# Two transformer blocks: the normalization between projections on one PSUM tile, five tiles ahead of it, and the gated product on VectorE

## The chip, the cores and the metric

One core of a Trainium2 chip runs the whole program. The metric is the device time of one execution in microseconds (us), lower is better.

## The reference

Input x is 256 tokens of 1024 features, float32. A first block (attention, a gated linear recurrence and a differential attention, merged by gates) and two layers of a second block follow each other. All of them end in the same way: an output projection is added to x, x is normalized, and a gated feed-forward part with a short causal convolution follows. For the second block:

```python
    mix = jnp.einsum('bsd,de->bse', merged, w_o)
    x = layer_norm(ALPHA * x + mix, ln1_g, ln1_b)
    up = causal_dwconv_2(jnp.einsum('bsd,df->bsf', x, w_up), ffn_conv_w)
    a, b = jnp.split(up, 2, axis=-1)
    ffn = jnp.einsum('bsf,fd->bsd', jax.nn.silu(a) * b, w_down)
    return layer_norm(ALPHA * x + ffn, ln2_g, ln2_b)
```

The first block has RMS norms (no mean), GELU in place of SiLU and a bias in the convolution. The feed-forward width is 2816, 22 tiles of 128, for the gate and as many for the value.

## The kernel before, in words

x lies in SBUF with the features on the partitions: 8 tiles (`x[:, k]`) of 128 features x 256 tokens. All weights come as one stream of 128 x 128 tiles in the order of use. A piece of 8 tiles (512 KB) is loaded from SP's queue into one of six raw buffers and split into a rounded part `whi` (ScalarE, L186) and a rest `wlo` (VectorE, L187), with five buffers each. `W.begin(t0, n)` splits what tiles t0 to t0+n need and up to two pieces more (L193). One product of 8 weight tiles with 8 activation tiles is 24 matmuls, since `mm3` (L342) multiplies hi by hi, hi by lo and lo by hi. Activations are split in the same way (`split`, L353): `hh` (ScalarE) and `hl` (VectorE) for x.

A scheduler orders the instructions of each engine: it takes the source's order as priority and its own estimates of readiness, so an instruction that is ready can pass one that comes earlier in the source. PSUM has eight tiles of 128 x 512 (`ps`); a tile is free when its last reader is done.

**The seam** (`seam`, L476) joins an output projection (`prev`), a norm and the first tiles of the next projection (`nxt`). For each of the 8 output tiles it adds the product to x (L886 or L889), splits x times the norm's gain into zh and zl (L509, L510) and adds x and its square to running sums (`Norm.add`, L390: squares on ScalarE, sums on GpSimd for m < 7, on VectorE for m = 7). The next projection does not wait for the norm: its first NAHEAD = 4 tiles are multiplied with zh and zl, which lack only the factor 1/std (and the mean's share), one value per token. After the first of these tiles TensorE adds the sums over the partitions (`stats`, L417 and L418). Then follows a chain of small steps of 128 x 256 (L423 to L432, L467 to L474): the square of the mean on ScalarE, the mean, the variance, 1/sqrt from ScalarE with one Newton step on VectorE. `apply` (L447) makes the normalized x, hh and hl from it, tile by tile. The first two centring subtractions run on VectorE, the others on GpSimd; the product with rstd on VectorE (L454, L457 or L439); gain and bias on ScalarE. Only then do the tiles that ran ahead leave PSUM, times rstd (L532); with a LayerNorm GpSimd adds the mean's term (L538). The rest of `nxt` is multiplied with hh and hl, up to two tiles side by side.

There are seven seams: one at the start without a projection ahead of it, five between, and one at the end, whose norm (`finish`, L434) writes the result out. Three have a projection of 8 tiles ahead of them (w_out, twice w_o), three the down projection of 22.

**The up projection** (`ffn_up`, L910) computes gate tile j and value tile j by turns. Evacuation of a tile: a scaled copy on ScalarE (L919, L921), two shifted multiply-adds on VectorE (L922, L923), for a gate the activation function on ScalarE (L926). Gate times value runs on GpSimd (L929), for the last pair on VectorE (L932). The split of the product into fh and fl (L355, L356) is put off to the next tile's evacuation (`late`, `settle`). The down projection reads fh and fl of all 22 tiles in order.

## Time and profile before

| | us |
|---|---|
| median of 3 runs | 1213.05 |
| lowest and highest run | 1207.31, 1213.48 |
| the profiled execution | 1208.3 |
| its span | 1206.3 |

The profile shows the one execution of 1208.3 us; its times count from the start of its span. PE is TensorE, PEld its weight loads, DVE is VectorE, ACT ScalarE, POOL GpSimd, SP the engine whose queue issues the loads. A start and a duration in a timeline are in us; neighbours on one engine overlap a little, since the next instruction begins while the last one drains. PEclk is the granted TensorE clock of a stretch, 1.00 being 2.4 GHz.

### The profile page before, as it was taken

The numbers are of one execution on the slowest core, as the hardware profiler recorded it, in microseconds if no ns is written. First come the engines' busy times: TensorE is split into PE (matmuls) and PEld (weight loads), VectorE is DVE, ScalarE is ACT, GpSimd is POOL, SyncE is SP. The second block draws the span as 40 slices with busy tenths as digits, with TensorE's granted clock in tenths as the row PEclk, the third lists the DMA queues.
The fourth block names the chain that finished last, engine by engine and source line by source line (L and its number), as shares of the span: only waits on it lengthen the run. The fifth ranks groups of instructions, "written<-read, shape, count | busy, mean of one in ns | idle before, by whom it ended". The sixth has DMA issues, their size and how long they took to land.

```text
span 1206.3 us, 25236 instructions
## 1 busy us (share of the span) xinstructions
PE 1165.5 (97%) x9928; PEld 1146.3 (95%) x9928; DVE 956.2 (79%) x1767; ACT 763.7 (63%) x1391; POOL 245.0 (20%) x233
## 2 busy tenths in 40 slices
PE   8999999999999999999999999999999998999895
PEld 8999899999999999999998999999999998999895
DVE  7989886797988856886789988757995888977754
ACT  7678566756767645676557766556776565855542
POOL 2022020001122200120023222222420042222122
PEclk9999999999999999999999999999999998999898
DMA  7654445475466665545554566664455554565541
GB/s 284 224 168 155 166 143 168 127 229 189 148 212 202 196 207 192 162 154 175 184 184 142 165 210 203 209 193 148 151 189 177 185 166 135 155 203 185 189 141 35
DMA packets 60486, 212.61 MB, mean 176 GB/s; under 512 B 6864, under 2 KB 9296, under 8 KB 60368
## 3 DMA queue, kind: packets, MB, share of 16 engines
q1 hardware_dynamic: 60080, 210.88, 54.3%
q8 instruction: 77, 1.26, 0.4%
q10 hardware_dynamic: 288, 0.14, 0.1%
q14 instruction: 41, 0.34, 0.1%
HBM read 209.94 MB, written 1.05 MB: 175 GB/s over the span
## 4 chain that ended last, share of the span: by engine, by line
PE 65%; DVE 17%; ACT 9%; issue 5%; POOL 3%; DMA 0%; SPq 0%; POOLq 0%; ACTq 0%; DVEq 0%
PE ps L344 20%; PE ps L343 20%; PE ps L345 20%; DVE wlo L187 7%; ACT whi L186 4%; POOL wrk L929 2%; DVE R L510 1%; DVE wrk L923 1%; DVE wrk L922 1%; ACT a_lg L580 1%; PE ps L563 1%; PE ps L760 1%; PE ps L761 1%; PE ps L759 1%; DVE wrk L454 1%
## 5 line engine op out<-in xcount | busy, mean ns | idle before, releaser
L187 DVE TENSOR_TENSOR wlo<-raw,whi 128x1024 fp32r<-128x1024 f32 (+1 forms) x401 | 496.3, 1240 | 118.5 <-ACT whi L186 113.1
L343 PE MATMUL ps<-hh,whi 128*128 128x256 f32 x1912 | 536.5, 281 | 5.1 <-ACT hh L461 3.6
L344 PE MATMUL ps<-hl,whi 128*128 128x256 f32 x1912 | 532.0, 279 | 3.2 <-DVE hl L462 3.1
L186 ACT CAST whi<-raw 128x1024 fp32r<-128x1024 f32 (+1 forms) x401 | 414.6, 1038 | 186.8 <-PE ps L344 135.5
L345 PE MATMUL ps<-hh,wlo 128*128 128x256 f32 x1912 | 531.3, 278 | 0.6 <-DVE wlo L187 0.4
L343 PEld LDWEIGHTS ps<-hh,whi 128*128 128x128 f32 x1912 | 361.6, 189 | 8.3 <-ACT hh L461 4.0
L344 PEld LDWEIGHTS ps<-hl,whi 128*128 128x128 f32 x1912 | 362.1, 190 | 4.4 <-DVE hl L462 4.0
L345 PEld LDWEIGHTS ps<-hh,wlo 128*128 128x128 f32 x1912 | 361.1, 189 | 1.0 <-DVE wlo L187 1.0
L343 PE MATMUL ps<-R,whi 128*128 128x256 f32 (+1 forms) x1180 | 330.2, 281 | 6.8 <-ACT R L355 3.8
L344 PE MATMUL ps<-R,whi 128*128 128x256 f32 (+1 forms) x1180 | 329.5, 280 | 5.2 <-DVE R L510 3.5
L345 PE MATMUL ps<-R,wlo 128*128 128x256 f32 (+1 forms) x1180 | 327.9, 279 | 0.4 <-DVE wlo L187 0.2
L343 PEld LDWEIGHTS ps<-R,whi 128*128 128x128 f32 x1180 | 223.6, 190 | 9.0 <-ACT R L355 4.5
L344 PEld LDWEIGHTS ps<-R,whi 128*128 128x128 f32 x1180 | 223.5, 189 | 7.5 <-DVE R L510 4.9
L345 PEld LDWEIGHTS ps<-R,wlo 128*128 128x128 f32 x1180 | 223.1, 189 | 1.3 <-DVE wlo L187 1.2
L929 POOL TENSOR_TENSOR wrk<-wrk 128x256 f32<-128x256 f32 x63 | 82.9, 1316 | 238.6 <-DVE wrk L923 150.3
L355 ACT CAST R<-wrk 128x256 fp32r<-128x256 f32 x89 | 36.0, 407 | 117.5 <-POOL wrk L929 95.3
L405 POOL TENSOR_TENSOR n_sq<-n_sq,n_q 128x256 f32<-128x256 f32 x42 | 39.5, 941 | 169.1 <-ACT n_q L396 167.9
L922 DVE SCALAR_TENSOR_TENSOR wrk<-ps,par,wrk 128x255 f32<-128x255 f32 x120 | 56.6, 476 | 17.3 <-ACT wrk L921 17.3
L356 DVE TENSOR_TENSOR R<-wrk,R 128x256 fp32r<-128x256 f32 x89 | 38.9, 440 | 27.0 <-ACT R L355 26.9
L923 DVE SCALAR_TENSOR_TENSOR wrk<-ps,par,wrk 128x254 f32<-128x254 f32 x120 | 57.1, 477 | 1.6
L611 POOL TENSOR_SCALAR a_lg<-a_lg,a_r 128x256 f32<-128x256 f32 x24 | 25.3, 1056 | 113.1 <-DVE a_r L586 60.9
L509 ACT ACTIVATE R<-x,par 128x256 fp32r<-128x256 f32 x48 | 23.8, 507 | 27.8 <-DVE x L889 16.0
(225 smaller groups left out, 1088.7 us busy)
## 6 DMA issues: line engine op xcount, KB each, us to landing
raw<-in_wst SPq DMA_DIRECT2D x395, 512.0 KB, 4.0
x<-in_xT SPq DMA_DIRECT2D x4, 256.0 KB, 4.8
out_y<-x SPq DMA_DIRECT2D x3, 256.0 KB, 2.2
cst<-in_cst SPq DMA_DIRECT2D x1, 406.0 KB, 8.9
raw<-in_wst SPq DMA_DIRECT2D x1, 384.0 KB, 5.5
par<-in_par SPq DMA_DIRECT2D x1, 312.5 KB, 8.5
raw<-in_wst SPq DMA_DIRECT2D x1, 256.0 KB, 2.7
out_y<-x SPq DMA_DIRECT2D x2, 128.0 KB, 2.0
```

The source lines that it names most:

```text
L186: self.nc.scalar.copy(hi[:, a:b], w[:, a:b])
L187: self.nc.vector.tensor_sub(lo[:, a:b], w[:, a:b], hi[:, a:b].bitcast(F32))
L343: T.matmul(out, sh, mh, start=first, stop=False, skip_group_check=skip)
L344: T.matmul(out, sh, ml, start=False, stop=False, skip_group_check=skip)
L345: T.matmul(out, sl, mh, start=False, stop=last, skip_group_check=skip)
L355: A.copy(hi, src)
L356: V.tensor_sub(lo, src, hi.bitcast(F32))
L405: e.tensor_add(self.sq, self.sq, q)
L611: (G if i else V).tensor_scalar(pe[:, c], pe[:, c], r[:, i:i + 1], None, op0=OP.mult)
L922: V.scalar_tensor_tensor(y[:, 1:], p[:, :S - 1], pr(cw, 44 + i), y[:, 1:], op0=OP.mult, op1=OP.add)
L923: V.scalar_tensor_tensor(y[:, 2:], p[:, :S - 2], pr(cw, i), y[:, 2:], op0=OP.mult, op1=OP.add)
L929: G.tensor_tensor(y, held.pop(j), y, op=OP.mult)
```

## The change

`stats` keeps the whole chain in the PSUM tile of the sums: the variance, the squared root and 1/std are written there, and each of these steps on VectorE reads at most one tensor from SBUF; the square of the root moves to ScalarE, and an activation of one column with the next phase's function (`func`) follows it. A copy of 1/std goes to SBUF (`rs`) for the tiles that ran ahead. Centring reads the sum from PSUM for the first two tiles; gain and bias of every second tile move to VectorE. In the seams after a projection of 8 tiles the running sums are added on VectorE. Five tiles run ahead instead of four; three of them leave PSUM after the fourth, sixth and eighth step of the normalization and two behind it, and the mean's term is added on VectorE through the PSUM tile of the sums. Two tiles follow side by side in the up projections (7 tiles belong to a seam instead of 5) and in `win` (7 instead of 6). The weight pieces are split at other places: one call ahead of the statistics, none more with the later tiles, and one piece each after the third and the sixth step (`more`). In the up projection every product of gate and value runs on VectorE.

```diff
-NWIN = 6
+NWIN = 7
...
-NAHEAD = 4
+NAHEAD = 5
...
+    def more(self):
+        if self.splits < min(self.npc, self.low + NPC):
+            self.split()
...
-        def add(self, m, last=False):
+        def add(self, m, last=False, e=None):
...
-            e = G if m < 7 else V
+            e = e or (G if m < 7 else V)
...
-            v = wrk()
+            self.rstd, self.s1p = q[:, :S], p[:, S:]
+            f, v, y = self.rstd, wrk(), wrk()
             if self.ln:
                 self.mu, m2 = tmp("n_mu", [P, S], 1), wrk()
...
+                A.activation(m2, self.s1p, AF.Square, scale=1.0 / D)
+                V.tensor_scalar(self.mu, self.s1p, 1.0 / D, None, op0=OP.mult)
+                V.scalar_tensor_tensor(f, f, 1.0 / D, m2, op0=OP.mult, op1=OP.subtract)
+                V.tensor_scalar(v, f, 0.0, LN_EPS, op0=OP.max, op1=OP.add)
             else:
-                V.tensor_scalar(v, p[:, :S], 1.0 / D, RMS_EPS, op0=OP.mult, op1=OP.add)
-            self.rstd, self.done = rsqrt(v, tmp("n_r", [P, S], 1))
-            if self.ln and not last:
-                self.nmr = tmp("n_nm", [P, S], 1)
-                V.scalar_tensor_tensor(self.nmr, self.mu, -1.0, self.rstd, op0=OP.mult, op1=OP.mult)
+                V.tensor_scalar(v, f, 1.0 / D, RMS_EPS, op0=OP.mult, op1=OP.add)
+            A.activation(y, v, AF.Abs_reciprocal_sqrt)
+            A.activation(f, y, AF.Square)
+            if self.func is not None:
+                A.activation(tbl, f[:, :1], self.func)
+            V.scalar_tensor_tensor(f, f, -0.5, v, op0=OP.mult, op1=OP.mult)
+            self.done = V.scalar_tensor_tensor(f, f, 1.5, y, op0=OP.add, op1=OP.mult)
+            if not last:
+                self.rs = tmp("n_r", [P, S], 1)
+                A.copy(self.rs, self.rstd)
+
+        def center(self, k, d):
+            if k < 2:
+                V.scalar_tensor_tensor(d, self.s1p, -1.0 / D, x[:, k], op0=OP.mult, op1=OP.add)
+            else:
+                G.tensor_sub(d, x[:, k], self.mu)
+
+        def affine(self, k, e):
+            g, b = self.g[:, k:k + 1], self.b[:, k:k + 1]
+            if k % 2:
+                V.tensor_scalar(x[:, k], e, g, b, op0=OP.mult, op1=OP.add)
+            else:
+                A.activation(x[:, k], e, AF.Identity, scale=g, bias=b)
...
-        def apply(self):
-            for k in range(NT):
...
+        def apply(self, k):
...
+                d = wrk()
+                self.center(k, d)
+                V.tensor_tensor(e, d, self.rstd, op=OP.mult)
+                self.affine(k, e)
...
             if prev:
-                norm.add(m, not nxt)
+                norm.add(m, not nxt, V if prev[0][1] == 8 else None)
...
+        at = 0 if prev else 2
         for i, mt in enumerate(ahead):
-            W.begin(mt["t0"], 8)
+            if i > at + 1:
+                W.begin(mt["t0"], 8, None, 0)
+            elif i <= at:
+                W.begin(mt["t0"], 8)
...
-            if i == (0 if prev else 2):
+            if i == at:
                 for m in range(0 if prev else NT):
                     norm.add(m)
+                W.begin(ahead[i + 1]["t0"], 8, mt["t0"])
                 norm.stats()
-                norm.apply()
-        for mt, p in zip(ahead, out):
+        ts, gbs = [], tmp("n_gb", [P, 16], 1)
+
+        def leave():
+
+            mt, p = ahead[len(ts)], out[len(ts)]
             t = mt["into"] if "into" in mt else wrk()
-            V.tensor_tensor(t, p[:, :S], norm.rstd, op=OP.mult)
+            V.tensor_tensor(t, p[:, :S], norm.rs, op=OP.mult)
+            gb = None
             if norm.ln:
-                gb = tmp("n_gb", [P, 2], 2)
+                gb = gbs[:, 2 * len(ts):2 * len(ts) + 2]
                 A.copy(gb, p[:, S:width])
-                u = wrk()
-                A.activation(u, norm.nmr, AF.Identity, scale=gb[:, 0:1], bias=gb[:, 1:2])
-                G.tensor_add(t, t, u)
+            ts.append((t, gb))
+        for k in range(NT):
+            norm.apply(k)
+            if k in (2, 5):
+                W.more()
+            if k in (3, 5, 7):
+                leave()
+        while len(ts) < len(ahead):
+            leave()
+        if norm.ln:
+            nmr = tmp("n_nm", [P, S], 1)
+            V.scalar_tensor_tensor(nmr, norm.mu, -1.0, norm.rs, op0=OP.mult, op1=OP.mult)
+        for mt, (t, gb) in zip(ahead, ts):
+            if norm.ln:
+                u = norm.s1p
+                A.activation(u, nmr, AF.Identity, scale=gb[:, 0:1], bias=gb[:, 1:2])
+                V.tensor_tensor(t, t, u, op=OP.add)
             if "evac" in mt:
                 mt["evac"](t)
...
-                elif j < FT - 1:
-                    G.tensor_tensor(y, held.pop(j), y, op=OP.mult)
-                    late.append(lambda: split(fh[j], fl[j], y))
                 else:
                     V.tensor_tensor(y, held.pop(j), y, op=OP.mult)
-                    split(fh[j], fl[j], y)
+                    late.append(lambda: split(fh[j], fl[j], y))
+                    if j == FT - 1:
+                        settle()
...
-    n1 = Norm(False, pr("norm_ffn_g", 0, 8), to_x=False)
+    n1 = Norm(False, pr("norm_ffn_g", 0, 8), to_x=False, func=AF.Gelu_apprx_tanh)
...
-    seam(outs("w_out", 0, 8, mg), add_x, n1, up[:5], (8, 6))
+    seam(outs("w_out", 0, 8, mg), add_x, n1, up[:7], (8, 6))
...
-    phase(up[5:])
+    phase(up[7:])
```

The two norms before an up projection in the second block ask for SiLU in the same way (and take `up[:7]`), the two before `win` ask for Exp; `finish` uses `center` and `affine` too.

## Rows read from the trace of the kernel before

**Rows 1.** The page: busy time, share of the span and instructions of each engine.
```profile
PE 1165.5 (97%) x9928; PEld 1146.3 (95%) x9928; DVE 956.2 (79%) x1767; ACT 763.7 (63%) x1391; POOL 245.0 (20%) x233
```

**Rows 2.** Windows: length, busy us (count) of PE, PEld, DVE, ACT, POOL; PEclk, DMA share, GB/s.
```profile
276.00:297.00 21.00, 19.49 (x166) 18.83 (x164) 18.41 (x25) 15.76 (x27) 5.08 (x6) 1.00 0.56 178
622.00:643.00 21.00, 19.83 (x163) 18.98 (x162) 19.57 (x28) 15.73 (x28) 14.25 (x12) 0.98 0.54 170
643.00:660.00 17.00, 15.49 (x116) 15.01 (x115) 15.28 (x30) 11.47 (x24) 5.00 (x7) 0.92 0.33 116
828.50:845.50 17.00, 15.28 (x112) 14.85 (x111) 16.25 (x33) 11.67 (x27) 6.89 (x8) 0.90 0.35 118
976.00:1001.50 25.50, 22.65 (x178) 22.01 (x177) 20.77 (x26) 15.37 (x26) 13.41 (x12) 0.93 0.54 170
1001.50:1019.00 17.50, 14.01 (x97) 13.51 (x95) 15.35 (x29) 10.98 (x23) 6.58 (x6) 0.80 0.31 96
1060.00:1120.00 60.00, 60.00 (x532) 60.00 (x531) 44.92 (x72) 34.34 (x60) 17.18 (x11) 1.00 0.58 188
1124.00:1142.00 18.00, 13.58 (x94) 12.57 (x93) 13.03 (x20) 10.17 (x17) 3.08 (x2) 0.81 0.62 202
```

**Rows 3.** TensorE's waits in the whole run: us in total, times, longest.
```profile
PE ps L343 <- ACT R L355: 3.8, 3, 2.8
...
PE ps L343 <- ACT hh L461: 3.6, 2, 2.8
...
PE ps L344 <- DVE R L510: 3.5, 6, 1.4
```

**Rows 4.** Timeline of POOL in layer 1's up projection: start, duration, [idle before].
```profile
1112.30 1.56 POOL L929 TENSOR_TENSOR wrk<-wrk 128x256 f32<-128x256 f32 x1 [4.27 <-DVE wrk L923]
...
1118.13 1.56 POOL L929 TENSOR_TENSOR wrk<-wrk 128x256 f32<-128x256 f32 x1 [4.27 <-DVE wrk L923]
```

**Rows 5.** Timeline of ACT in layer 1's up projection.
```profile
1113.89 0.41 ACT L355 CAST R<-wrk 128x256 fp32r<-128x256 f32 x1 [1.99 <-POOL wrk L929]
```

**Rows 6.** Line 932: duration ns min/median/max, first and last start.
```profile
L932 DVE TENSOR_TENSOR wrk<-wrk x3: 424/425/426, 419.1 to 1135.5; 128x256 f32<-128x256 f32 x3
```

**Rows 7.** Groups of DVE by line, 1060 to 1118: busy us, mean ns, idle before.
```profile
L187 DVE TENSOR_TENSOR wlo<-raw,whi 128x1024 fp32r<-128x1024 f32 x21 | 25.5, 1216 | 0.1
...
L923 DVE SCALAR_TENSOR_TENSOR wrk<-ps,par,wrk 128x254 f32<-128x254 f32 x21 | 10.1, 479 | 0.4
...
L922 DVE SCALAR_TENSOR_TENSOR wrk<-ps,par,wrk 128x255 f32<-128x255 f32 x20 | 9.6, 479 | 13.0 <-ACT wrk L921 13.0
```

**Rows 8.** Timeline of ACT after the statistics of layer 1's first norm.
```profile
1001.58 0.39 ACT L423 ACTIVATE wrk<-ps 128x256 f32<-128x256 f32 x1 [4.01 <-PE ps L418]
```

**Rows 9.** Timeline of DVE after the same statistics.
```profile
1002.00 0.42 DVE L424 TENSOR_SCALAR n_mu<-ps 128x256 f32<-128x256 f32 x1 [2.88 <-ACT wrk L423]
...
1003.31 1.76 DVE L187 TENSOR_TENSOR wlo<-raw,whi 128x1024 fp32r<-128x1024 f32 x1
...
1009.55 0.41 DVE L454 TENSOR_TENSOR wrk<-wrk,n_r 128x256 f32<-128x256 f32 x1
```

**Rows 10.** Groups of ACT by line, whole run: busy us, mean ns, idle before.
```profile
L401 ACT ACT_TABLE_LOAD x6 | 7.7, 1283 | 0.1
```

**Rows 11.** Lines 454 and 532: duration ns min/median/max, first and last start.
```profile
L454 DVE TENSOR_TENSOR wrk<-wrk,n_r x24: 409/412/966, 650.2 to 1012.9; 128x256 f32<-128x256 f32 x24
...
L532 DVE TENSOR_TENSOR wrk<-ps,n_r x17: 409/414/421, 29.6 to 1030.3; 128x256 f32<-128x256 f32 x17
```

**Rows 12.** Timeline of DVE in the last norm.
```profile
1193.57 0.42 DVE L424 TENSOR_SCALAR n_mu<-ps 128x256 f32<-128x256 f32 x1 [1.29 <-ACT wrk L423]
...
1199.28 1.77 DVE L439 TENSOR_TENSOR wrk<-x,n_r 128x256 f32<-128x256 f32 x5
...
1202.42 0.41 DVE L442 TENSOR_SCALAR x<-wrk,par 128x256 f32<-128x256 f32 x1
```

**Rows 13.** Line 510: duration ns min/median/max, first and last start.
```profile
L510 DVE SCALAR_TENSOR_TENSOR R<-x,par,R x48: 471/610/967, 4.2 to 998.3; 128x256 fp32r<-128x256 f32 x48
```

63 lines of the change are left out of this document (26 added, 37 removed).

## Prediction

> **What bounds the kernel now.** I read four views in this order: the page's busy shares, TensorE's own waits, a table of windows, and the timelines where the table shows lost time. TensorE is busy 97% of the span [rows 1], so only time that it loses can be won. In a stretch without waits it starts 532 matmuls in 60.00 us, 0.1128 us each, at the full 2.4 GHz [rows 2]. So each window's lost time is its length less 0.1128 us times its count. That gives:
> - at the ends of the output projections, before the statistics: 21.0 - 166 x 0.1128 = 2.3 us (first block, 276 to 297), 2.6 us (second block layer 0, 622 to 643) and 5.4 us (layer 1, 976 to 1001.5);
> - after the statistics of the three LayerNorms that a projection follows: 3.9 us (643), 4.4 us (828.5) and 6.6 us (1001.5), together 14.9 us;
> - at the start of the last down projection: 18.0 - 94 x 0.1128 = 7.4 us (1124).
>
> Part of this is the clock: PEclk is 0.80 in the 1001.5 window and 0.81 in the 1124 window, after TensorE had stood still, so 0.4 of 17.5 us, some 7 us, ran at 1.2 GHz and cost half of that. TensorE's waits name the same places [rows 3]: hh (L461), the split of the residual R (L510), and the split of the gated product (ACT R L355).
>
> **The up projection and the last down projection.** In layer 1 the gate times value step on GpSimd starts at 1112.30 and again at 1118.13 [rows 4]: 5.83 us for a pair of tiles, while TensorE needs 48 x 0.1128 = 5.41 us. The evacuation therefore loses 0.42 us per pair. GpSimd's product lasts 1.56 us, and ScalarE, which splits it, stands 1.99 us before that split [rows 5]; behind it in ScalarE's queue wait the next evacuation and the next weight split. TensorE runs ahead, reaches the last rows of the down projection first and stands there. The change makes the product on VectorE, where the last pair's already is, at 0.425 us [rows 6]. VectorE then has, per pair, two weight splits at 1.22, four convolution steps at 0.48 [rows 7], one split and one product at 0.43: 5.2 us of durations, and since neighbours overlap by 0.08 us about 4.6 us of queue, against 5.41. What covers it is this margin; without it the last wait stays. The last tile then needs, after its matmuls, some six steps of 0.42 to 0.48 us, 2.7 us, and TensorE asks for it only 63 x 0.1128 = 7.1 us into the down projection. I take the whole 7.4 us; bounds 4 us (the other end of a lag halved) and 7.4.
>
> **The LayerNorm chain.** In layer 1 it runs from ScalarE's square of the mean at 1001.58 [rows 8] to the first product x times rstd at 1009.55 [rows 9]: 7.97 us, with a weight split of 1.76 us inside. After the change: square 0.42 (VectorE's first step ended a 2.88 us wait with it today too; both read the same PSUM tile [rows 9]); three VectorE steps at 0.45 with handover, 1.35; reciprocal root and square on ScalarE, 0.84; then the preload of the next function's table. That preload reads the column which VectorE's next step overwrites, so VectorE and the chain wait for it: 1.28 [rows 10] and a small activation, at most 0.39 like the square of [rows 8]; two VectorE steps, 0.9. Sum 5.2 us; 5.6 if the copy of rstd to SBUF goes ahead of the first product. So 2.4 to 2.8 us are won in layer 1, mostly from steps that no longer stretch: a product of two SBUF operands takes 412 ns but up to 966, one with a PSUM operand never over 421 in 17 [rows 11]. The table load is not new, it sat in the evacuation, off TensorE's path; here it is on the chain. The Trainium skill, "ScalarE: Activation LUTs", section "Table sets: the hidden batching unit", prices such a load at about 2.7 us and so speaks against it; the trace's 1.28 us decides. By the page's figure each of three chains would be 1.4 us longer and my estimate 1199 us.
>
> A fifth tile ahead adds 24 x 0.1128 = 2.7 us of TensorE work before hh is asked for, so the wait for the first hh goes. What is late next is the pair that follows side by side: it asks for two weight pieces at once, 4 x 2.7 + 0.6 = 11.4 us after the statistics, and the second is split only after the sixth step of the normalization. In strict order VectorE has by then 6 products, 6 splits hl, 3 affine steps and 2 tiles leaving PSUM, 17 steps at 0.34 (five products in 1.77 us [rows 12]), 5.8 us, plus two weight splits at 1.2: 5.2 + 5.8 + 2.4 = 13.4, 2 us late; 1 us late if one split slips into the chain as the one at 1003.31 did. I charge 2.0 us per seam, half speed included: 14.9 - 3 x 2.0 = 8.9 us won. Bounds: 0 and 14.9. Hh itself is asked for every 0.68 us by the pair instead of every 0.34 us, so it is not late again by much. The splits moved by the new calls issue the same 512 KB loads from SP's queue, as many as before and a few us earlier or later; six raw buffers cover that, and if not a wait for a load joins the 2 us.
>
> After it, each of the five tiles adds its bias term through one PSUM buffer, ScalarE and VectorE by turns, and TensorE does not wait for that while leaving tiles free their banks. The two RMS seams get a chain longer by table load and square, less one VectorE step, about 1.6 us; the fifth tile's 2.7 us covers it. Cost 0, at worst 3 us together.
>
> **The projections before the statistics.** Six to twelve additions per seam move from GpSimd to VectorE, 12 x 0.34 = 4.1 us; in return the residual's split falls from its median 0.61 and maximum 0.97 us to its minimum 0.47 [rows 13], up to 8 x 0.5 = 4.0 us. VectorE is already busy 20.77 of 25.5 us in the 976 window [rows 2]. A wash: 0, bounds 5 us lost and 5 us won.
>
> **The last norm.** From 1193.57 to the first product at 1199.28 [rows 12] are 5.7 us. After: three VectorE steps and one centring step (1.7 us), root and square (0.9), two steps (0.9): 3.5, 2.2 us won. VectorE's rest has two affine steps more, 12 x 0.34 = 4.1 against 1202.83 - 1199.28 = 3.55. Net about 1.7 us; bounds 0.5 and 2.4.
>
> **Sum.** 7.4 + 8.9 + 0 + 0 + 1.7 = 18.0 us. The profiled execution took 1208.3 us (span 1206.3), so it would take 1190.3. It lies 4.75 us under the median of the runs, 1213.05, whose lowest is 1207.31; against the median I predict 1195.
>
> **Rivals.**
> - *Everything is covered*: no wait is left after the statistics and VectorE without GpSimd beside it is also faster ahead of them. For: 966 against 421 ns [rows 11]. Against: VectorE's 13.4 us above. 6 us and some 2 us more: 1187.
> - *The order does not come about*: a scheduler places instructions by its own estimates (the split at 1003.31 stands in the chain though its call comes later in the source). Then tiles leave PSUM and pieces are split at other places than the source says, and the three LayerNorms lose as much as today: 1195 + 8.9 = 1204.
> - *VectorE bounds the up projection*: its 5.2 us of durations per pair are only 0.2 us under 5.41, and today it also idles 13.0 us in 58 before the first convolution step of a tile [rows 7]. Then the last wait stays: 1195 + 7.4 = 1202.
> - *Slower: the pair's second weight piece comes behind the whole normalization in all five seams.* Then 25 steps at 0.34 instead of 17 stand before it: 5.2 + 8.5 + 2.4 = 16.1, 4.7 us late, and a fall of the clock with it, which I price at 1.7 us (half of what the 1001.5 window lost): 5 x 6.4 = 32 us against the 24 us of all the gains. That is 8 us slower, 1221. It decides from 24/5 = 4.8 us per seam on, clock included. Against it: splits have so far slipped forward, not back [rows 9].
>
> **How the numbers follow.** Chances: forecast 0.60, everything covered 0.12, order 0.12, VectorE bound 0.10, slower 0.06. The range leaves out the slower case and the corners of the others: 1185 (everything covered, 2 us of bounds) to 1209 (order and half of the down projection's wait together). A measurement of this kernel can tell about 0.5%, 6 us, from no change. Faster: 0.60 + 0.12 + 0.07 + 0.06 = 0.85, less 0.01 for the forecast's own tail, 0.84; within 0.5%: 0.10; slower: 0.06.
>
> **What would show it.** Right: GpSimd's product gone and VectorE's product near 0.43 us; no TensorE wait for ACT R L355's successor at the last down projection and PEclk 1.00 there; a LayerNorm chain of 5 to 6 us with a 1.28 us table load in it; a wait of 1 to 2 us at the pair, named by the weight split (wlo). Wrong: a count in the windows after the statistics as low as today's, VectorE near 100% in the up projection, or waits longer than 4 us at the pair.

## The result and the profile after

The changed kernel takes 1194.38 us (median of 4 runs, 1188.71 to 1196.26) against 1211.22 us (4 runs, 1207.31 to 1213.48) for the kernel before: ratio 0.988, 95% interval 0.985 to 0.991. Predicted were 1195, range 1185 to 1209. The profiled run took 1194.4 us (span 1192.6), 13.9 us less than the profiled run of before; the sum of the prediction was 18.0 on that scale. The total is close, but several of its terms are not, and two large ones were missing.

The page's first part, which answers to [rows 1]: VectorE has taken over what GpSimd gave up, TensorE is a little shorter.

```profile
PE 1163.8 (98%) x9928; PEld 1146.4 (96%) x9928; DVE 970.5 (81%) x1887; ACT 769.4 (65%) x1401; POOL 109.7 (9%) x128
```

TensorE's waits in the whole run of after (us in total, times, longest). The lines for hh after a LayerNorm and for the split of the gated product ahead of the down projection [rows 3] are gone, and the residual's wait (3.5) has halved. New at the top are waits of the attention (K2 and V2 are the tiles of keys and values of one attention of a layer; L606 is the scores, L1011 the turn of V2).

```profile
PE ps L606 <- ACT R L359: 2.2, 1, 2.2
...
PE ps L348 <- DVE R L530: 1.7, 4, 0.7
PE ps L606 <- DVE R L360: 1.7, 1, 1.7
PE ps L349 <- DVE wlo L187: 1.2, 4, 0.4
...
PE ps L1011 <- ACT wrk L1004: 1.0, 1, 1.0
```

Windows of after, with the columns of [rows 2]. Each is cut so that it holds the same matmuls, counted from the start, as a window of before; so the two lengths can be compared directly. (The counts in two rows differ by one or two where a matmul lies across an edge.) The fifth row has no partner in [rows 2]; it stands behind, from the trace of before.

```profile
275.13:294.40 19.27, 19.05 (x165) 18.77 (x164) 17.52 (x31) 16.11 (x27) 0.00 (x0) 1.00 0.60 192
622.09:641.82 19.73, 19.06 (x163) 18.63 (x161) 19.24 (x38) 15.55 (x28) 0.00 (x0) 1.00 0.56 177
641.82:655.64 13.82, 13.82 (x117) 13.79 (x116) 11.46 (x26) 9.77 (x18) 4.37 (x6) 1.00 0.42 146
825.47:838.82 13.35, 13.35 (x113) 13.32 (x111) 11.41 (x24) 9.85 (x20) 5.29 (x6) 1.00 0.40 151
838.82:865.28 26.46, 21.59 (x175) 20.92 (x174) 25.95 (x60) 16.85 (x37) 4.86 (x5) 0.94 0.45 159
975.61:997.18 21.57, 20.97 (x177) 20.57 (x176) 20.45 (x40) 16.08 (x27) 0.19 (x1) 1.00 0.54 179
997.18:1008.88 11.70, 11.64 (x97) 11.44 (x96) 10.47 (x20) 9.03 (x16) 4.86 (x6) 1.00 0.57 181
1051.20:1113.63 62.43, 62.43 (x533) 62.43 (x532) 56.70 (x97) 40.70 (x69) 0.00 (x0) 1.00 0.64 210
1117.63:1128.35 10.72, 10.72 (x94) 10.72 (x92) 6.73 (x9) 5.12 (x8) 0.00 (x0) 1.00 0.56 190
```

```profile
845.50:865.50 20.00, 20.00 (x176) 19.73 (x175) 18.85 (x34) 12.53 (x24) 9.53 (x8) 1.00 0.58 185
```

Read against [rows 2], the table gives:
- ahead of the statistics: 21.00 to 19.27, 21.00 to 19.73, 25.50 to 21.57, together 6.9 us won;
- behind the three LayerNorms: 17.00 to 13.82, 17.00 to 13.35, 17.50 to 11.70, together 12.6 us won;
- right after the second of them, where layer 1 starts: 20.00 to 26.46, 6.5 us lost;
- last down projection: 18.00 to 10.72, 7.3 us won;
- the row 1051.20: 533 matmuls in 62.43 us, with TensorE busy throughout and PEclk 1.00. Before, 532 took 60.00 us. Nothing waits there, yet each step is 4% longer.

The last norm, VectorE's timeline in after [rows 12]. From the mean (L430) to the first product (L463) it takes 3.25 us, before 5.71; from the mean to the end of the span 1192.6 - 1181.85 = 10.75 us against 1206.3 - 1193.57 = 12.73, so 2.0 us are won.

```profile
1181.85 0.42 DVE L430 TENSOR_SCALAR n_mu<-ps 128x256 f32<-128x256 f32 x1 [1.29 <-ACT wrk L429]
...
1185.10 1.08 DVE L463 TENSOR_TENSOR wrk<-x,ps 128x256 f32<-128x256 f32 x3
```

The sum is 6.9 + 12.6 - 6.5 + 7.3 + 2.0 = 22.3 us; the spans differ by 13.7. The starts of the matmuls show where the rest went. From 1030 to 1180 us, 1270 of them in a row follow each other every 117.8 instead of 113.3 ns (5.65 us, of which 0.4 is in the last window above). A short stretch of that pace at 658 us costs 0.8, and at 532.6 us the granted clock is half for 3.4 us, which costs 2.1 us by the count of matmuls. That leaves 0.4 us net of items that the windows do not hold. Among them: the kernel before has the half clock at 171.3 us, which costs it 1.6 us and which this execution of after does not have; after loses 0.9 us behind the first block's norm (below) and as much right behind the windows of the first and third LayerNorm.

### The profile page after: what moved, and what is told of

Same layout as the page of the kernel before. It is cut to its first block, busy times and chain, and to the rows that moved or that the text cites. A ratio compares the mean times of both kernels' runs of the same rounds, so it can differ in the third digit from the quotient of the medians.

```text
span 1192.6 us, 25172 instructions
## 1 busy us (share of the span) xinstructions
PE 1163.8 (98%) x9928; PEld 1146.4 (96%) x9928; DVE 970.5 (81%) x1887; ACT 769.4 (65%) x1401; POOL 109.7 (9%) x128
## 3 DMA queue, kind: packets, MB, share of 16 engines
q8 instruction: 78, 1.28, 0.4%
## 4 chain that ended last, share of the span: by engine, by line
PE 75%; DVE 14%; ACT 7%; issue 3%; POOL 1%; DMA 0%; SPq 0%; ACTq 0%; DVEq 0%; POOLq 0%
PE ps L347 24%; PE ps L348 24%; PE ps L349 24%; DVE wlo L187 5%; ACT whi L186 2%; PE ps L606 1%; PE ps L803 1%; PE ps L804 1%; DVE R L530 1%; PE ps L802 1%; DMA raw<-in_wst 0%; PE ps L636 0%; ACT a_lg L623 0%; DVE wrk L720 0%; DVE R L748 0%
## 5 line engine op out<-in xcount | busy, mean ns | idle before, releaser
L186 ACT CAST whi<-raw 128x1024 fp32r<-128x1024 f32 (+1 forms) x401 | 416.0, 1041 | 272.2 <-PE ps L348 221.8
L347 PE MATMUL ps<-hh,whi 128*128 128x256 f32 x1872 | 523.8, 282 | 2.1 <-ACT hh L483 0.5
L348 PE MATMUL ps<-hl,whi 128*128 128x256 f32 x1872 | 520.3, 279 | 0.9 <-DVE hl L484 0.8
L349 PE MATMUL ps<-hh,wlo 128*128 128x256 f32 x1872 | 518.8, 279 | 0.8 <-DVE wlo L187 0.8
L347 PEld LDWEIGHTS ps<-hh,whi 128*128 128x128 f32 x1872 | 352.0, 189 | 5.4 <-ACT hh L483 0.7
L349 PEld LDWEIGHTS ps<-hh,wlo 128*128 128x128 f32 x1872 | 353.2, 189 | 1.3 <-DVE wlo L187 1.2
L347 PE MATMUL ps<-R,whi 128*128 128x256 f32 (+1 forms) x1220 | 340.0, 279 | 2.0 <-ACT whi L186 1.0
L348 PE MATMUL ps<-R,whi 128*128 128x256 f32 (+1 forms) x1220 | 338.7, 278 | 1.7 <-DVE R L530 1.7
L349 PE MATMUL ps<-R,wlo 128*128 128x256 f32 (+1 forms) x1220 | 338.0, 278 | 0.6 <-DVE wlo L187 0.4
L347 PEld LDWEIGHTS ps<-R,whi 128*128 128x128 f32 x1220 | 229.1, 188 | 3.4 <-ACT whi L186 1.4
L348 PEld LDWEIGHTS ps<-R,whi 128*128 128x128 f32 x1220 | 229.4, 188 | 2.9 <-DVE R L530 2.7
L349 PEld LDWEIGHTS ps<-R,wlo 128*128 128x128 f32 x1220 | 229.6, 188 | 1.4 <-DVE wlo L187 1.4
L409 POOL TENSOR_TENSOR n_sq<-n_sq,n_q 128x256 f32<-128x256 f32 x24 | 21.8, 907 | 292.2 <-ACT n_q L400 291.2
L964 ACT ACTIVATE wrk<-ps,par 128x256 f32<-128x256 f32 x78 | 35.7, 471 | 6.9 <-PE ps L349 6.9
L623 ACT ACTIVATE a_lg<-a_lg,a_mx 128x128 f32<-128x128 f32 x64 | 28.5, 447 | 11.3 <-DVE a_mx L617 8.2
```

The costliest lines, as they stand in the source:

```text
L186: self.nc.scalar.copy(hi[:, a:b], w[:, a:b])
L347: T.matmul(out, sh, mh, start=first, stop=False, skip_group_check=skip)
L348: T.matmul(out, sh, ml, start=False, stop=False, skip_group_check=skip)
L349: T.matmul(out, sl, mh, start=False, stop=last, skip_group_check=skip)
L623: A.activation(pe[:, c], lg[:, c], AF.Exp, bias=mx[:, i:i + 1], scale=slope, accum_out=sm[:, i:i + 1])
L964: A.activation(y, p, AF.Copy, scale=pr(cw, 88 + i))
```

## What the new wait is

ScalarE, then VectorE, then TensorE in after, at the start of layer 1 (timeline: start, duration, idle before).

```profile
847.04 0.57 ACT L580 ACTIVATE ps<-n_nm,n_gb 128x256 f32<-128x256 f32 x1 [0.56 <-DVE xcr L581]
...
849.98 0.57 ACT L580 ACTIVATE ps<-n_nm,n_gb 128x256 f32<-128x256 f32 x1 [0.78 <-DVE gbr L581]
...
851.77 0.35 ACT L1004 COPY wrk<-ps 128x256 f32<-128x256 f32 x1
...
855.22 0.41 ACT L359 CAST R<-wrk 128x256 fp32r<-128x256 f32 x1 [1.90 <-DVE wrk L997]
```

```profile
848.07 0.40 DVE L581 TENSOR_TENSOR gbr<-gbr,ps 128x256 f32<-128x256 f32 x1
848.41 1.21 DVE L187 TENSOR_TENSOR wlo<-raw,whi 128x1024 fp32r<-128x1024 f32 x1
849.54 0.40 DVE L581 TENSOR_TENSOR gbr<-gbr,ps 128x256 f32<-128x256 f32 x1
...
851.01 0.40 DVE L581 TENSOR_TENSOR wrk<-wrk,ps 128x256 f32<-128x256 f32 x1
...
852.70 0.45 DVE L994 STREAM_SHUFFLE wrk<-wrk 128x256 f32<-128x256 f32 x1
```

```profile
852.17 0.44 PE L1011 MATMUL ps<-ident,wrk 128*128 128x128 f32 x2 [1.02 <-ACT wrk L1004]
857.55 0.44 PE L606 MATMUL ps<-R,R 64*128 64x128 f32 x4 [2.19 <-ACT R L359]
859.65 0.73 PE L606 MATMUL ps<-R,R 64*128 64x128 f32 x8 [1.66 <-DVE R L360]
```

The bias terms of the five tiles ahead all go through the one PSUM tile. So ScalarE can't write the next (L580) before VectorE has added the last (L581), and VectorE makes a weight split in between: 848.07 to 849.54, 1.47 us a round. K2, which before the change was one of the pair and left PSUM directly, is now the fifth tile, behind all five rounds; its rope (the rotary embedding) starts at 852.70. V2's copy (L1004) stands behind the same rounds in ScalarE's queue. TensorE meets first the turn of V2, then the scores that read K2, and waits three times; the half clock of 3.4 us follows.

## Experiments

Twelve runs. As stretches at 117.8 ns come at different places and not in every run, each profiled time is also given without it: the number of matmuls in its stretches of over 500, times 4.45 ns, is taken off. That is worked out from the starts of the matmuls in each trace.

```
run           profiled us   matmuls at 117.8 ns (from us)     without    ratio to before, 95% interval
before        1208.3        0                                 1208.3
after         1194.4        1270 (1030)                       1188.7     0.988  0.985 to 0.991
after_again   1201.6        1248 (680), 1423 (1019)           1189.8     0.987  0.982 to 0.992
u_sbuf        1190.9        1419 (659)                        1184.5     0.980  0.976 to 0.983
win4          1184.8        0                                 1184.8     0.979  0.975 to 0.984
win4u         1189.6        630 (244)                         1186.8     0.975  0.971 to 0.980
win4ug        1193.9        0                                 1193.9     0.984  0.980 to 0.988
sums_pool     1206.0        1272 (1040)                       1200.3     0.993  0.989 to 0.996
prod_pool     1195.0        811 (1031)                        1191.4     0.987  0.983 to 0.991
chain_sbuf    1200.3        1833 (293), 1233 (1037)           1186.6     0.987  0.981 to 0.994
nofunc        1200.3        1223 (681), 1226 (1040)           1189.4     0.990  0.984 to 0.996
reset         1196.1        1433 (1012)                       1189.7     0.984  0.980 to 0.988
prod_only     1208.2        1591 (296)                        1201.1     0.988  0.984 to 0.992
sums_only     1208.2        1254 (680)                        1202.6     0.991  0.987 to 0.995
```

Two profiles of one kernel (after, after_again) then differ by 1.1 us. What the column still holds is stretches of 3.4 us at half the granted clock at 131, 171 and 533 us, which come in some profiles and not in others: none in prod_pool and chain_sbuf, two in win4u, win4ug, sums_pool, prod_only and sums_only, one in each of the rest. One of them costs 1.6 to 2.1 us by the count of matmuls (171.3 us in before, 532.6 us in after), so differences of 2 us in that column mean nothing.

The ratios stand against executions of before made beside each run, whose median was 1211.22 us for after, 1215.54 for u_sbuf, win4, sums_pool and prod_pool, 1218.55 for prod_only, sums_only, reset and win4u, and 1210.93 for the other four; ratios of different groups are therefore comparable only to about 0.6%. The column without the slow pace leaves a cost out, it does not say that the cost has nothing to do with the edit (see the last run).

**u_sbuf**

```diff
-                u = norm.s1p
+                u = wrk()
```

> One line of the changed kernel: the bias term u of each tile that ran ahead goes to an SBUF buffer of its own again instead of the norm's PSUM tile. In the changed kernel's profile TensorE stands 1.3, 2.5 and 1.9 us at 851 to 860 us (start of layer 1: transposes of V2, first scores) and then has the half clock from 860.3 to 863.7, together 6.4 us lost against the kernel before by the count of matmuls. Theory: ScalarE's next u has to wait until VectorE has added the last one, since all five use one tile, so each round takes one weight split and one add (1.47 us) and K2's rope and V2's copy stand behind five of them. Then the five adds follow each other, K2's rope starts some 3 us earlier, and 4 to 6 us come back: about 1189 us with the pace of the profiled run (117.8 ns per matmul from 1030 us on), 1183 without it. Rival: the rounds are not the cause, K2 is late because it now runs ahead and leaves in the normalization's queue rather than as one of the pair: then the gaps stay and the time is 1194 (1189).

Measured 1190.03 us (4 runs, 1188.68 to 1190.86). The same matmuls as in the fifth row above, and a stretch at the slow pace in the same profile:

```profile
843.22:863.93 20.71, 19.95 (x176) 19.54 (x174) 20.71 (x46) 14.62 (x33) 5.57 (x5) 1.00 0.43 144
700.00:760.00 60.00, 60.00 (x511) 60.00 (x511) 54.30 (x91) 37.30 (x66) 0.00 (x0) 1.00 0.69 209
```

20.71 instead of 26.46 us: 5.8 come back, the half clock included. The five bias terms now stand in one row on ScalarE (848.22 to 850.80). Counted from the start of the window, K2's rope begins on ScalarE after 8.4 us (851.64) instead of 12.6 (851.44 in after). Without the rounds through the one tile the wait is gone; the rival, as I had put it, falls. The slow pace came at another place, 659 to 827 us, where the first profile had only the short stretch to 680, and not from 1030 us on.

**win4**

```diff
-NWIN = 7
+NWIN = 6
...
-        seam(outs("w_down_2", l, FT, FX), add_alpha_x, n, nxt[0] if nxt else [], (7, 1) if nxt else store)
+        seam(outs("w_down_2", l, FT, FX), add_alpha_x, n, nxt[0] if nxt else [], (7, 1) if nxt else store, 4)
...
-    seam(outs("ffn_down", 0, FT, FX), add_x, n2, w0[0], (7, 1))
+    seam(outs("ffn_down", 0, FT, FX), add_x, n2, w0[0], (7, 1), 4)
```

> The changed kernel with four tiles ahead instead of five in the two seams that lead into a layer of the second block (K2 and V2 are the pair again, as before the change); u still goes through the one PSUM tile. Theory (serial rounds): K2 and V2 don't stand behind the rounds as data any more but on the same queues, so part of the gap at 851 to 860 stays; 2 to 3 of the 6.4 us come back, and the wait for hh after the statistics (some 1 to 2 us) returns in this seam: 1192 to 1194. Rival (K2's place in the order): the gap goes, 6 us come back less 1 to 2 us for hh: 1189 to 1190.

Measured 1188.82 us (4 runs, 1184.77 to 1190.93).

```profile
824.99:839.74 14.75, 13.51 (x113) 13.28 (x111) 12.83 (x29) 10.05 (x21) 5.26 (x6) 1.00 0.40 136
839.74:859.30 19.56, 19.56 (x175) 19.29 (x174) 19.56 (x43) 14.13 (x29) 5.36 (x5) 1.00 0.46 145
```

The gap goes here too (19.56), all of it, and the fifth tile's worth shows in the row above: 14.75 against 13.35 us, 1.4 us. So K2's place behind five rounds is needed for the wait as well: rounds and place make it together, and taking away either is enough. The theory of u_sbuf, as I had put it for this run, gave too little.

**win4u**: the edits of win4 and u_sbuf together.

> Both repairs of the new wait at the start of layer 1 together: four tiles ahead in the seams into a layer of the second block (the run win4: 1188.8), and the bias term u in SBUF (the run u_sbuf: 1190.0). Theory: both lift the same wait, so little adds up: 1187 to 1189 with matmuls at 113.3 ns, up to 6 us more where a stretch falls to 117.8 ns. Rival: u in SBUF also takes the backlog out of the up projections' start, where TensorE waits for a free PSUM tile at 680 and 1030 us: 1184.

Measured 1188.47 us (4 runs, 1184.62 to 1191.56). As expected, little adds up. Its ratio lies below that of after, but against other executions of before. In the same group stands reset, the changed kernel but for nine transposes, with 1198.13 us; so win4u is very likely faster than the changed kernel too, by 2 to 3 us at equal pace. TensorE still waits for a free PSUM tile (1.5 us at 1029 us, as in u_sbuf), so the rival falls.

**win4ug**: win4u with the addition on GpSimd again.

```diff
-                V.tensor_tensor(t, t, u, op=OP.add)
+                G.tensor_tensor(t, t, u, op=OP.add)
```

> Four tiles ahead in the seams into a layer of the second block and the bias term u in SBUF (as win4u), and its addition back on GpSimd, as before the change. Between 1016 and 1040 us VectorE was busy 23.9 of 24 us, and TensorE waited 1.7 us at 1029 us for a PSUM tile. Theory: five additions fewer on VectorE per seam shorten that backlog, the wait at 1029 us falls below 0.5 us: 1 to 2 us faster than win4u at the same pace of matmuls (1182 to 1184 without a slow stretch). Rival: GpSimd's additions (0.74 to 1.57 us each in the kernel before) stretch VectorE's steps beside them and the tiles leave later: 2 us slower.

Measured 1193.32 us (4 runs, 1189.75 to 1194.06), 7 us behind win4u at the same pace. The wait for a PSUM tile at 1029 us is gone (one of 0.5 us for a weight split comes at 1041), but a longer one comes at 676.7 us:

```profile
PE ps L349 <- DVE wlo L187: 3.7, 4, 2.7
```

It is worse than the rival's 2 us and not for its reason: GpSimd's five additions end at 670.8 us. VectorE, without the additions in its queue, goes through the tiles' convolutions from 672.13 to 678.45 with no weight split among them (win4u has two by then, at 672.36 and 674.62), and the split that TensorE needs comes late. The half clock follows, from 679.6 us. The order of VectorE's queue changed with the engine of one small step.

**sums_pool**

```diff
-                norm.add(m, not nxt, V if prev[0][1] == 8 else None)
+                norm.add(m, not nxt)
```

> The changed kernel with the running sums of squares and of x ahead of the statistics back on GpSimd (nothing else undone). My prediction called their move a wash (0, bounds 5 us either way). By the count of matmuls the changed kernel gained 1.8, 1.2 and 4.2 us ahead of the statistics of the three output projections. Theory: all of that is the sums' doing, GpSimd's additions stretch VectorE's residual split while both run; then some 6 to 7 us are lost: 1201 (median residual split 0.61 us again). Rival: the gain ahead of the statistics comes from elsewhere (splits of the weight stream at other places, GpSimd free of the product): then 1194 to 1196.

Measured 1205.71 us (10 runs, 1197.75 to 1212.17).

```profile
277.56:298.67 21.11, 19.60 (x165) 18.91 (x164) 18.41 (x25) 15.92 (x27) 5.08 (x6) 1.00 0.58 177
624.85:645.44 20.59, 19.41 (x163) 18.69 (x161) 19.25 (x28) 15.71 (x28) 14.25 (x12) 1.00 0.53 167
980.34:1005.75 25.41, 22.56 (x177) 21.93 (x176) 20.78 (x26) 15.37 (x26) 13.41 (x12) 0.93 0.56 169
```

Against 19.27, 19.73 and 21.57 us, 6.5 of the 6.9 us are lost again. Behind the last of them, 997.18:1008.88 in after, another 1.7 us go (13.37 for 11.70). Of the 11.6 us between the two profiles without the slow pace, the rest is mostly half clocks: one more at the start, and one of 6.8 instead of 3.4 us at 862 us, with a wait at 1040 us. The residual split takes 608 ns in the median instead of 479 (both below). The theory holds.

```profile
L530 DVE SCALAR_TENSOR_TENSOR R<-x,par,R x48: 474/608/969, 4.3 to 1002.6; 128x256 fp32r<-128x256 f32 x48
```

```profile
L530 DVE SCALAR_TENSOR_TENSOR R<-x,par,R x48: 468/479/964, 4.4 to 994.0; 128x256 fp32r<-128x256 f32 x48
```

**sums_only**: the kernel before, with the same edit made instead of undone (`add` gets the argument `e`).

> The kernel before with one part of the change alone: the running sums ahead of the statistics of the output projections on VectorE. My prediction: a wash, 0 with bounds of 5 us. Undoing this part in the changed kernel cost some 11 us (run sums_pool against the profiled run of after, both with the slow pace of matmuls at the end). Theory now: it is worth 6 us ahead of the statistics and some 3 to 5 us behind them, where TensorE enters the norm with the clock at full and VectorE's queue emptier: 1198 to 1202 on the scale of the profiled 1208.3. Rival: alone it moves only the stall from ahead of the statistics to behind them, since the chain there stays: 1205 to 1208.

Measured 1207.43 us (7 runs, 1198.7 to 1211.66).

```profile
978.47:1000.06 21.59, 20.99 (x178) 20.58 (x176) 20.51 (x40) 16.11 (x27) 0.20 (x1) 1.00 0.57 181
1000.06:1013.91 13.85, 12.28 (x97) 11.55 (x96) 13.15 (x26) 9.23 (x19) 5.12 (x6) 1.00 0.39 115
1121.57:1139.90 18.33, 14.16 (x93) 13.32 (x92) 12.38 (x21) 10.64 (x17) 2.26 (x2) 0.82 0.68 212
```

The whole gain ahead of the statistics in layer 1 is there with this edit alone (21.59), and 3.65 us behind them (17.50 to 13.85), the half clock of before in that window [rows 2] included. The stall of the last down projection stays (18.33). Without the slow pace it takes 1202.6 us, at the edge of what the theory gave.

**prod_only**: the kernel before, with the product on VectorE for all tiles, as in the diff of the change.

> The kernel before with one part of the change alone: gate times value on VectorE for every tile, its split held back as in the change. My prediction gives this part the whole stall at the last down projection: 7.4 us, so about 1201 where the profiled run of before had 1208.3, and a last down projection with no wait for the split of the product. Rival, from the run with the product put back on GpSimd, where the stall did not return (its matmuls ran at 117.8 instead of 113.3 ns each there, so TensorE asked later): VectorE's pace in the up projection is what counts, and without the other edits a stall stays: 1205 to 1208.

Measured 1205.15 us (10 runs, 1197.46 to 1217.83); without the slow pace the profiled run takes 1201.1.

```profile
1131.71:1142.02 10.31, 10.31 (x93) 10.31 (x92) 6.80 (x9) 5.22 (x8) 0.00 (x0) 1.00 0.60 199
```

18.00 to 10.31, 7.7 us: in the kernel before this edit alone removes the stall.

**prod_pool**: the change with the product on GpSimd again for all tiles but the last.

> The changed kernel with the gate times value product back on GpSimd for all but the last tile of each up projection. Theory of the prediction: the evacuation then takes 5.83 us per pair of tiles against TensorE's 5.41, the lag piles up until the last down projection and TensorE stands there 7 us, with the clock at half after it: 1194 + 7 = 1201. Rival: the stall came from the last tile's order of splits and not from GpSimd's pace, and the changed kernel's other edits have removed it anyway: 1195 or less.

Measured 1199.29 us (4 runs, 1194.99 to 1201.95).

```profile
1119.86:1130.88 11.02, 10.89 (x93) 10.69 (x92) 9.03 (x14) 6.76 (x11) 1.56 (x1) 1.00 0.68 196
```

The stall did not return here, though the products come 5.83 us apart again (1108.51, 1114.34). At the slow pace of this stretch TensorE needs 48 x 0.1171 = 5.62 us for a pair (533 matmuls in 62.42 us), so the lag grows by 0.2 us per pair instead of 0.4, some 2 us less by the end. That is not the whole reason. In before, the product starts 6.3 us after the value tile's last matmul where the spacing of 5.83 us sets in (1065.67 us), and 10.6 us after it at the last one on GpSimd (1129.79). Here it is 3.5 us (1061.88) and 5.3 (1120.17). With 0.2 us more for each of these ten pairs it would be some 7.4: the products enter the stretch with 2.8 us less lag, and the changed kernel's other edits, or the slow pace since 1031 us, have done that. So what the move of the product is worth inside the changed kernel is not shown. In layer 0 of before GpSimd's products come 5.30 us apart (701.60, 706.90), and no such stall follows there: a product on GpSimd is too slow only in the order that the queues take in layer 1, and what makes that order was not looked for.

**chain_sbuf**

```diff
...
-            A.activation(f, y, AF.Square)
+            V.tensor_tensor(a, y, y, op=OP.mult)
...
-            V.scalar_tensor_tensor(f, f, -0.5, v, op0=OP.mult, op1=OP.mult)
-            self.done = V.scalar_tensor_tensor(f, f, 1.5, y, op0=OP.add, op1=OP.mult)
-            if not last:
-                self.rs = tmp("n_r", [P, S], 1)
-                A.copy(self.rs, self.rstd)
+            V.scalar_tensor_tensor(a, a, -0.5, v, op0=OP.mult, op1=OP.mult)
+            self.rstd = self.rs = tmp("n_r", [P, S], 1)
+            self.done = V.scalar_tensor_tensor(self.rs, a, 1.5, y, op0=OP.add, op1=OP.mult)
```

> The changed kernel with the reciprocal root computed in SBUF again (square on VectorE, rstd in SBUF, the variance's own buffer), the rest as changed: five tiles ahead, centring of two tiles from PSUM, preload of the table. Theory now: the chain's place in PSUM matters little for TensorE because the fifth tile covers the chain; in the last norm products with two SBUF operands beside GpSimd's centring take up to 0.97 us instead of 0.41, so 1 to 2 us are lost there, and little elsewhere: 1 to 3 us slower than the changed kernel at the same pace. Rival (my prediction): 2.4 to 2.8 us per LayerNorm come from it, and without it waits for hh return in each of three seams: 5 to 8 us slower.

Measured 1198.16 us (4 runs, 1188.0 to 1203.55); 1186.6 at 113.3 ns, not slower than after (1188.7), which has one half clock more. Behind the LayerNorms TensorE loses nothing:

```profile
646.07:659.90 13.83, 13.83 (x117) 13.80 (x116) 13.11 (x28) 9.68 (x19) 4.86 (x6) 1.00 0.31 103
...
1000.26:1011.62 11.36, 11.36 (x97) 11.36 (x96) 10.64 (x22) 8.64 (x15) 5.29 (x6) 1.00 0.48 141
```

The last norm is slower: 1198.5 - 1186.12 = 12.4 us from the mean to the end, against 10.75. So what this edit undoes (the PSUM tile, and the square on ScalarE) is worth 1.6 us, all of it in the last norm, where no matmul covers it.

**nofunc**: the four `func=` arguments left out.

> The changed kernel without the preload of the next function's table inside the norm chain (the load falls to the first evacuation again, as before the change). Theory of the prediction: the load is 1.28 us on the chain plus 0.17 us for its small activation, so in the three LayerNorms the first product comes 1.3 to 1.5 us earlier; TensorE is covered there by the fifth tile, so the time stays within 2 us: 1186 to 1196 with the stretch of slower pace or without. Rival: the chain's length is what TensorE pays at the pair after the statistics or in the backlog at 1030 us; then 2 to 4 us are won.

Measured 1200.13 us (4 runs, 1193.88 to 1205.79); 1189.4 at 113.3 ns, as after. The chains did not get 1.3 us shorter: from ScalarE's square to the first product they take 7.8, 8.4 and 7.1 us against 7.9, 7.9 and 7.6. Weight splits fill the place. The time follows the theory (it stays within 2 us), the chain does not.

**reset**

```diff
...
+            if i == 6:
+                w = ps()
+                for j in range(3):
+                    T.transpose(w[:, j * P:(j + 1) * P], ident, ident)
...
-    phase(up[7:])
+    even(up[7:])
...
```

> The changed kernel with three small transposes of the identity, whose result nobody reads, issued on TensorE once in each up projection, ahead of its 14th tile. In the profile of after, matmuls without any wait start every 113.3 ns up to 1030 us and every 117.8 ns from there to the end, 1270 in a row (5.65 us in all); the change of pace comes with a single step of 180 ns, at the full granted clock. In other runs such a stretch begins with another wait and ends with a wait or with the three transposes of an attention head. Theory: it is a phase between matmul and weight load that a short wait sets and another irregular step clears; then the transposes clear it, the second part of the up projection and the down projection run at 113.3 ns, and the time is 1188.5 to 1190 (three times some 0.3 us for the transposes). Rival: it is a clock or power limit of the chip in that stretch; then the pace stays at 117.8 ns and the time is 1195.

Measured 1198.13 us (4 runs, 1194.59 to 1201.79). The transposes ran at 1031 us, and the pace stayed slow before and after them:

```profile
1050.00:1110.00 60.00, 60.00 (x512) 60.00 (x511) 54.87 (x93) 39.16 (x66) 0.00 (x0) 1.00 0.71 211
```

My theory that any such step clears it falls. That the chip sets a limit, as the rival has it, is not shown by this either.

**after_again**: the changed kernel once more.

> The changed kernel once more, unchanged, on the same chip as the next three. Theory: its profile differs from the first one only in where a stretch of matmuls at 117.8 ns lies, if there is one (at 113.3 ns everywhere 1187 to 1189, with one stretch up to 1196); TensorE's wait of some 6 us at 851 to 863 us is there again. Rival: the stretch from 1030 us on belongs to the changed kernel's order of work; then it is there again at the same place.

Measured 1196.86 us (4 runs, 1191.77 to 1201.64).

```profile
700.00:760.00 60.00, 60.00 (x512) 60.00 (x511) 53.75 (x91) 37.71 (x68) 0.00 (x0) 1.00 0.61 204
844.07:871.89 27.82, 23.04 (x175) 22.27 (x174) 26.53 (x63) 17.12 (x38) 4.85 (x5) 0.88 0.43 152
1060.00:1120.00 60.00, 60.00 (x511) 60.00 (x511) 54.33 (x91) 39.64 (x67) 0.00 (x0) 1.00 0.67 208
```

The new wait is there again (27.82 us for the same matmuls, with 6.8 us at half the clock instead of 3.4). There are two stretches of the slow pace instead of one: that from 680 us is new, so the theory is right that such a stretch can come or not, and that from 1019 us is close to the first profile's, so the rival is right as well. The table of runs bears it out: a stretch of over 500 begins between 1012 and 1041 us in seven of the eight profiles in which u goes through PSUM (all but win4), in none of the three with u in SBUF (win4ug has a short one, 219 matmuls from 1016 us), and in none of the three of before and its two variants. So this one goes with the changed kernel's order in layer 1, though not in a way that I can name. The half clock at 532.6 us did not come again here, behind the same two waits of 0.24 and 0.50 us; but win4ug (532.8), sums_only (532.5) and prod_only (540.9) have it at the same place. So it can come there in any of these kernels, in four of fourteen profiles.

## Why the prediction came out right, and where it was wrong

**Up projection and last down projection: right.** 7.4 us forecast, 7.3 measured (7.7 at equal pace), PEclk 1.00 there, and prod_only shows that in the kernel before the product alone does it. VectorE's product is at 423 ns in the median, and TensorE waits for nothing from 1117 to 1130 us. The reading behind it, 5.83 us for a pair on GpSimd, holds for the second half of layer 1 alone (prod_pool).

**The LayerNorm chain: more was won behind it than forecast, and the reason was wrong.** The step that failed is "Sum 5.2 us; 5.6 if the copy ...": the chain takes 7.6 us in layer 1, from 996.06 on ScalarE to 1003.62 on VectorE, hardly less than the 7.97 of before. The steps that the sum lists have about the length that it gives them. What it left at nothing is 0.5 us in which the root waits on ScalarE behind a weight split (997.39), and 2.0 us from the last step (1001.59) to the product: a weight split on VectorE, a centring and the mean's term. Another split, at 998.47, costs nothing, since VectorE then waits for the table load (tbl) anyway:

```profile
996.48 0.42 DVE L430 TENSOR_SCALAR n_mu<-ps 128x256 f32<-128x256 f32 x1 [0.17 <-ACT wrk L429]
...
998.47 1.74 DVE L187 TENSOR_TENSOR wlo<-raw,whi 128x1024 fp32r<-128x1024 f32 x1 [0.65 <-ACT whi L186]
...
1000.69 0.43 DVE L439 SCALAR_TENSOR_TENSOR ps<-ps,wrk 128x256 f32<-128x256 f32 x1 [0.48 <-ACT tbl L438]
...
1001.63 1.40 DVE L187 TENSOR_TENSOR wlo<-raw,whi 128x1024 fp32r<-128x1024 f32 x1
...
1003.62 0.41 DVE L473 TENSOR_TENSOR wrk<-wrk,ps 128x256 f32<-128x256 f32 x1
```

chain_sbuf and nofunc show that the chain's form and the table load in it move TensorE by nothing that the profile resolves. So what removed the waits must be what else stands in the seam. Shown are the fifth tile (1.4 us in win4) and the sums (3.65 us in layer 1 in sums_only, 1.7 in sums_pool). Without either, most of the gain is still there: 14.75 us in win4 against 17.00, 13.37 in sums_pool against 17.50. By elimination that is left to the pair, to the tiles that leave between the steps and to the weight pieces split at other places; these were not separated, and this part of the cause stays open.

The table load itself is 1.28 us, and its small activation starts 1.29 us after the load's start (999.20, 1000.49). The Trainium skill, "ScalarE: Activation LUTs", section "What ACT_TABLE_LOAD costs", states about 1283 ns for the load and about 2.66 us with a drain; the first figure agrees with this trace; the second does not show here, since from the end of the square (999.18) to the small activation only 1.31 us pass.

**The 2.0 us per seam at the pair: wrong.** TensorE's four waits for a weight split at L349 make 1.2 us in the whole run, 0.4 at most. The step that failed is "In strict order VectorE has by then ... 17 steps": the weight splits came earlier than that order has them, three of them by 1005.5 us, two of these ahead of the first product. The 6 us charged did not fall due: 12.6 won instead of 8.9.

**The projections ahead of the statistics: wrong, outside the bounds.** "A wash: 0, bounds 5 us" measured 6.9 us won. I charged VectorE the full 4.1 us of the additions and set the shorter residual splits against it. But before the change VectorE stood idle for 25.5 - 20.77 = 4.7 us of the last of these windows [rows 2], and with the additions its busy time over the same matmuls is 20.45 us, so they went into such time, while TensorE's wait for the residual split fell from 3.5 [rows 3] to 1.7 us. How the rest of the 6.9 us divides was not separated. The rows say that GpSimd's additions stretch the split: 608 ns beside them, 479 without. The Trainium skill, "SBUF — State Buffer", section "SBUF: two separate sides", says that a VectorE step with two inputs in SBUF and a GpSimd step that reads SBUF lock each other out. The split reads x and its own upper part from SBUF, so the trace agrees.

**What the prediction did not have: the start of layer 1.** It says that each of the five tiles adds its bias term through one PSUM buffer "and TensorE does not wait for that while leaving tiles free their banks". That looked at banks only. It did not follow who reads the fifth tile: K2, whose rope and scores come next in the same queues. 6.5 us were lost; two runs undo one half of the cause each, and both get them back (5.8 and 6.9).

**RMS seams and last norm.** For the RMS seams 0 was forecast, at worst 3 us lost. Behind the first block's w_out norm 0.9 us are lost: the same 100 matmuls take 12.18 us (313.57 to 325.75) instead of 11.33, with a wait of 0.4 us for a weight split in them. Behind the other RMS norm by the count nothing is lost up to 525 us, and whether the half clock at 533 us has to do with the change is open, since a variant of before has it too (sums_only). The last norm won 2.0 us for a forecast 1.7.

**The total.** At equal pace the change is worth 1208.3 - 1188.7 = 19.6 us, or 18.5 by the second profile (each of the three has one half clock that comes and goes); the sum was 18.0. It came out by errors of opposite sign: 6.9 + 3.7 + 0.3 us more than forecast, 6.5 less at the start of layer 1, 2.1 less by the half clock. That the median came within 0.6 us of the forecast is luck: four of the sum's terms were off by 2 us and more, or missing. The first profile has another 5.65 us of slow pace. Of the three profiles of before and its variants two have such a stretch as well, but the one from 1030 us on goes mostly with the changed order, and the prediction had no term for it. The upper end of the range, 1209, does not come out of its parts: 1204 and half of 7.4 are 1207.7.

## What to carry to other kernels

When a tile is moved into a group that is held back, follow it to its reader: a shared scratch tile makes the holders leave one after the other, at the price of whatever else the engines do between (1.47 us a round here, of which 0.40 was the addition itself). Moving an elementwise step between VectorE and GpSimd should be costed by what the other engine's steps stretch to beside it, not by its own duration alone. And where the same kernel differs by several us between executions, compare stages that hold the same matmuls, not totals.

## What the runs showed of the hardware

TensorE has two paces here at one granted clock. Without any wait, and with PEclk 1.00, matmuls start every 113.3 ns or every 117.8 ns, in stretches of up to 1833. Of the 14 profiles, 11 have a stretch of over 500, at different places, one or two each, at 2.8 to 13.6 us per execution. Every long one begins at a step that was longer than usual (the one of after at a single step of 180 ns, some others behind a wait or at the statistics), and it can outlast three transposes in its midst. What sets it and what ends it is not settled; that seven of eight kernels with nearly the same order around 1030 us have one there says that the order of work has a part in it, that the stretches from 659 to 681 us come in one profile of a kernel and not in the next says that it is not all. One trait can be read: in a slow stretch one of the three weight loads that take turns lasts 192 ns in the mean, the others 188; in a fast one all three last 188. Which one it is differs: that of wlo in after from 1030 us on and in sums_only, that of whi for hl in after_again and u_sbuf, that of whi for hh in prod_only and in the first stretch of chain_sbuf. Groups of weight loads of after (1070 to 1110 us), then after_again (700 to 760), both in a slow stretch, then before (1070 to 1110), in a fast one:

```profile
L349 PEld LDWEIGHTS ps<-hh,wlo 128*128 128x128 f32 x114 | 21.9, 192 | 0.0
L347 PEld LDWEIGHTS ps<-hh,whi 128*128 128x128 f32 x114 | 21.4, 188 | 0.0
```

```profile
L348 PEld LDWEIGHTS ps<-hl,whi 128*128 128x128 f32 x170 | 32.7, 192 | 0.0
```

```profile
L345 PEld LDWEIGHTS ps<-hh,wlo 128*128 128x128 f32 x118 | 22.2, 188 | 0.0
```
